# Norm sums behind the first products, recurrent value transposes one block later, and eight banks for the out blocks, in a two-layer hybrid encoder

## The chip, the core and the metric

The kernel runs on one core of a Trainium2 chip. A core has a matrix engine (TensorE, PE in the rows), three engines for element-wise work (VectorE: DVE; ScalarE: ACT; GpSimd: POOL), and SyncE (SP), which starts most of the transfers here. Each engine works through its own list of instructions in order, and waits there for what other engines or transfers have to deliver. TensorE writes its sums to PSUM, which has eight banks, and another engine has to read a bank out before it can take a new sum. What is measured is the time of one execution on the device, in microseconds; lower is better.

## The reference, cut to what matters

The model is an encoder of two layers (width 1024) on 656 tokens: one stream of 528 (16 learned meta tokens and 512 of the prompt) and eight running streams of 16. All is float32. Cut from the reference:

```python
h = rmsnorm(x, p['g_mix'])
proj = h @ p['w_in']                                   # 1024 -> 3072
qa, ka, va, glu, zf, ic, qc, gc = jnp.split(proj, offs, axis=-1)
oa = diff_attention(qa, k_all, v_all, ...)             # 4 heads
ob = jax.nn.silu(layernorm(causal_dwconv(ga * sigmoid(gb), ...)))   # 256 channels
oc, S_new = hgrn2(qc, log_f, kc, ic, S0)               # 4 heads, gated recurrence
x = x + jnp.concatenate([oa, ob, oc], axis=-1) @ p['w_out']
h2 = rmsnorm(x, p['g_ffn'])
gate, val = jnp.split(h2 @ p['w_up'], 2, axis=-1)      # 1024 -> 2 x 2816
gate_c, ffn_new = causal_dwconv(gate, ffn_past, ...)   # width 3
x = x + (jax.nn.gelu(gate_c) * val) @ p['w_down']      # 2816 -> 1024

def rmsnorm(x, g):
    return x * lax.rsqrt(jnp.mean(x * x, axis=-1) + EPS) * g
```

The factor `rsqrt(...)` of a token is the same for all columns of its row. A product can therefore be made from `x * g` before the factor is known, and be multiplied by it afterwards. The kernel calls this factor r.

## The kernel before, in words

Activations lie transposed, 128 features on the partitions and 656 tokens along the row, in two halves of 328 tokens (`CA`; 322 in the later stages of layer 1, `CB`). Float32 accuracy is reached by splitting each operand into a high and a low part and adding three products: high by high, high by low, low by high (`mm3`, three matmuls for each 128-row step). ScalarE makes the high part (a cast), VectorE the low part (a subtraction). For weights these are `whi`, `wlo` (four rotating buffers) or `ghi`, `glo` (buffers of their own); for activations `hi_h`, `lo_h`.

The sums in PSUM come from two pools of names: `PD` has three of the eight banks, `PB` five, and `PX` goes around all eight.

A layer starts with a group of six products (three column blocks by two halves, `gemm_group`, sums `e0` to `e5`), which need no r: r is applied when VectorE evicts them (`evict_r`). r itself comes from `norm_r`: VectorE and GpSimd add the squares of the eight blocks of x, TensorE sums these over the partitions (`np_h`, two matmuls of four passes in all), ScalarE takes the reciprocal root, and VectorE refines it in three steps (`rt_h`, twice, and `r_h`). 21 more column blocks follow one by one (`d_0_i03` and so on), and between them the attention heads (`attention`), the recurrent heads (`hgrn`, two pairs) and the convolution advance as generators: each `yield` hands on to the next block. In `hgrn` the values of a pair of heads are transposed on TensorE into the banks `hvp` and `hvq`.

Then comes the out projection in two passes, six of eight input blocks (`d_oa`) and the last two (`d_ob`). After each out block of the second pass VectorE adds the sum to x (`add_x`) and, between these additions, makes the splits of x for the FFN (`split`, `lo_h`).

The FFN starts with another group of six (`e_u`: two gates and one value block) and `norm_r` for its own r (`r_h2`). In `factors` the whole x is scaled by r on VectorE (eight blocks), GpSimd makes sums of quarters of it (`ft`, `fu`), and ScalarE and VectorE split these into factors (`fh`) for Strassen's scheme: seven products in place of eight for all later gates and values (`strassen`). The two gates of the group are evicted by `plain_gate` (`gp`), which frees banks `e0` to `e3`. Two more plain gates (`d_g02`, `d_g03`) with weights of their own (`wg`) and a value block (`d_v01`) stand ahead of the Strassen products (`d_v010` the first).

The program is written in the order of the blocks; a list scheduler lays out each engine's list from it, by what is ready and which bank or buffer is free. So the order of the source sets the order on the engines only in part, and the order of the lists is shown below where it matters.

Of the kernel before, what the change touches and what calls it, by code (L numbers as in the profile page):

```python
# [37 lines left out]
NPG = 2  # L38
# [9 lines left out]
CA, CB, CC = ((0, 328), (328, 656)), ((12, 334), (334, 656)), ((16, 336), (336, 656))  # L48
# [108 lines left out]
def trunk_kernel(ctx: ExitStack, tc: tile.TileContext, i: dict, o: dict, depth: int = 2):  # L157
# [14 lines left out]
    def S(name, dt=F32):  # L172
        return slots.tile([128, T], dt, tag="S", name=name)
# [4 lines left out]
    def PB(name):  # L178
        return psb.tile([128, 512], F32, tag="b", name=name)
# [29 lines left out]
    onesd = const.tile([128, 3, 128], F32, name="onesd")  # L209
# [93 lines left out]
    def norm_r(ones, srcs, nm, cc=CA):  # L303

        r = S(f"r_{nm}")
        t = S(f"rt_{nm}")
        for c, (a, b) in enumerate(cc):
            ps = PB(f"np_{nm}{c}")
            n = b - a
            for j, s in enumerate(srcs):  # L310
                PE.matmul(ps[:, :n], lhsT=ones, rhs=s[:, a:b], start=j == 0, stop=j == len(srcs) - 1)
            A.activation(out=r[:, a:b], in_=ps[:, :n], func=AF.Abs_reciprocal_sqrt, bias=epsb, scale=1.0)
            A.activation(out=t[:, a:b], in_=r[:, a:b], func=AF.Square)
            V.scalar_tensor_tensor(out=t[:, a:b], in0=ps[:, :n], scalar=EPS, in1=t[:, a:b], op0=ALU.add, op1=ALU.mult)
        a, b = cc[0][0], cc[-1][1]
        V.scalar_tensor_tensor(out=r[:, a:b], in0=t[:, a:b], scalar=-3.0, in1=r[:, a:b], op0=ALU.add, op1=ALU.mult)
        return r
# [47 lines left out]
    def weights(w, k0, kt, own=False):  # L365
        return w_split(w_load(w, k0, kt), kt, 0, own)
# [14 lines left out]
    def gemm(units, ks, rhs, nm, cc=CA, P=PD):  # L381

        return [gemm1(units, ks, rhs, f"{c}_{nm}", cc[c], P) for c in range(2)]

    def gemm_group(unit_lists, ks, rhs, nm, cc=CA):

        ps = [[PD(f"e0_{nm}"), PD(f"e1_{nm}")], [PD(f"e2_{nm}"), PB(f"e3_{nm}")], [PB(f"e4_{nm}"), PB(f"e5_{nm}")]]
        last = len(ks) - 1
        for k in range(len(ks)):
            for m, units in enumerate(unit_lists):  # L390
                for c in range(2):
                    mm3(ps[m][c], units[k], rhs[ks[k]], cc[c], k == 0, k == last)
        return ps

    def evict_r(ps, r, nm):
        t = SE(nm)
# [4 lines left out]
    sq_acc = {}  # L401
# [325 lines left out]
    def hgrn(l, p, got, mix):  # L727
# [3 lines left out]
        f = S(f"f{l}{p}")  # L731
# [7 lines left out]
        while ("i", p) not in got:  # L739
            yield  # L740
        iv = got["i", p]
        vt = S(f"hvt{l}{p}")
        ps = PB(f"hvp{l}{p}")
        for c in range(4):
# [57 lines left out]
        for c in range(2):  # L802
            ps = PB(f"hd{l}{p}{c}")
            PE.matmul(ps[:, :HC], lhsT=b64, rhs=prod[:, HV[c]], start=True, stop=True)
            V.scalar_tensor_tensor(out=od[:, HV[c]], in0=ps[:, :HC], scalar=64.0, in1=iv[:, HV[c]], op0=ALU.mult, op1=ALU.mult)
        ps = PB(f"hd{l}{p}2")
# [44 lines left out]
        ps = PB(f"hkp{l}{p}")  # L851
# [12 lines left out]
        for hh in range(2):  # L864
            pr = slice(64 * hh, 64 * hh + 64)
            ps = PB(f"hsi{l}{p}{hh}")
# [16 lines left out]
        ps = PB(f"hsc{l}{p}")  # L883
# [222 lines left out]
    ks8 = list(range(8))  # L1106
    for l in range(depth):
# [6 lines left out]
        got, mix = {}, {}  # L1114
        if l == 0:
            hs = []
# [8 lines left out]
            w3 = []  # L1125
            start["on"] = True
            for m in range(8):
                hs.append(split(xs[m], par("g_mix", m), f"h{l}{m}"))
                if m == 0:
                    w3 = [w_split(raws[n], 4) for n in range(3)]  # L1130
                if m == 3:
                    w3 = [w3[n] + w_split(raws[n], 8, 4, True) for n in range(3)]
            for m in range(8):
                sq_add(m, E=V)
            start["on"] = False
        r = norm_r(onesd[:, 0], [sq_acc["t"]], f"h{l}")
        ps3 = gemm_group(w3, ks8, hs, f"i{l}")
        with ExitStack() as behind:
            if l == 0:
                for e in (mybir.EngineType.DVE, mybir.EngineType.Activation):  # L1140
# [1 line left out]
            nxt = weights(w[col[3]], 0, 8)  # L1142
# [16 lines left out]
        for n in range(3, 24):  # L1159
            advance(front)  # L1160
            ps = gemm(nxt, ks8, hs, f"i{l}{n}")
            got[order[n]] = evict_r(ps, r, f"e{l}{n}")
            if n < 23:
                nxt = weights(w[col[n + 1]], 0, 8)
# [8 lines left out]
        cx, cy = (CB, CC) if l == depth - 1 else (CA, CA)  # L1173
        ka, kb = KORD[:6], KORD[6:]
# [3 lines left out]
        nxt = weights(wo[0], 0, 6)  # L1178
        for k in ka:
            mix[k] = split(*mix[k], f"mx{l}{k}")  # L1180
        for m in range(8):
            advance(front)
            x_in(m, xsrc)
            ps = gemm(nxt, ka, mix, f"oa{l}{m}", cx)
            add_x(m, ps, cx)
            nxt = weights(wo[m + 1], 0, 6) if m < 7 else weights(wo[0], 6, 2)
# [6 lines left out]
        hs = []  # L1193
        wu = i["w_up"][l]
        w3 = [weights(wu[n], 0, 8, True) for n in (0, 1, NFF)]
        for m in range(8):
            ps = gemm(nxt, kb, mix, f"ob{l}{m}", cx)
            add_x(m, ps, cx)
            x_out(m)
            sq_add(m, (cx[0][0], T))  # L1200
            hs.append(split(xs[m], par("g_ffn", 8 * l + m), f"h2{l}{m}", cx[0][0]))
            if m < 7:
                nxt = weights(wo[m + 1], 6, 2)
        r = norm_r(onesd[:, 0], [sq_acc["t"]], f"h2{l}", cx)
        ps3 = gemm_group(w3, ks8, hs, f"u{l}", cx)
        gout = S(f"gout{l}")[:, :NFF * 18].rearrange("p (f n) -> p f n", f=NFF)
        wd = i["w_down"][l]
        a0, cw = cy[0][0], cx[0][1] - cx[0][0]
# [11 lines left out]

        for ft in range(2):
            plain_gate(ft, ps3[ft])
        wg = [weights(wu[ft], 0, 8, True) for ft in range(2, 2 + NPG)]
        for ft in range(2):
            ps = ps3[2] if ft == 0 else gemm(weights(wu[NFF + 1], 0, 8), ks8, hs, f"v{l}1", cx, PB)
            a, av = gates.pop(ft)
# [120 lines left out]
        if l < depth - 1:  # L1347
            hs = []
            w3 = [weights(i["w_in"][l + 1][col[n]], 0, 8, True) for n in range(3)]
# [7 lines left out]
    ks = list(range(f0, f0 + nf))  # L1357
    wl = [weights(wd[m], f0, nf, True) for m in range(WA)]
    for c, (a, b) in enumerate(CF):
# [3 lines left out]
        for m in range(8):  # L1363
            if c == 0 and m < 8 - WA:
                wl.append(weights(wd[m + WA], f0, nf, True))
            ps = gemm1(wl[m], ks, gts, f"fin{c}{m}", (a, b))
# [5 lines left out]
        r = norm_r(onesd[:, 0], [sq_acc["t"]], f"fin{c}", ((a, b),))  # L1372
# [22 lines left out]
```

## Time and profile before

| | |
|---|---|
| median of 3 runs | 1721.53 us (1720.11 to 1721.71) |
| profiled execution | 1721.48 us, of which the span 1719.7 |
| TensorE busy | 1634.3 us, 95% |
| VectorE busy | 1320.1 us, 77% |
| ScalarE busy | 827.7 us, 48% |
| GpSimd busy | 573.0 us, 33% |
| mean granted TensorE clock | 0.983 of full |
| chain that ended last | TensorE 67%, VectorE 22%, issue 5% |

The span is the time from the first to the last instruction, and the rest of the execution lies around it. Busy times are sums over the span; an engine that is idle waits for a transfer or another engine. The chain follows the work that ended last back to the start, at each step to what released it, and gives the shares of the span by engine. The times in the rows below are counted from the start of the span. Layer 0 goes from 0 to about 865 us, its FFN from about 398.

### The profile page before, as it was taken

Reading aid. Unit: us, or ns where it says so; the run is one execution under the profiler, and the core shown is the slowest. Engines: PE = TensorE matmul, PEld = TensorE weight load, DVE = VectorE, ACT = ScalarE, POOL = GpSimd, SP = SyncE. Lnnn points to the kernel's source line nnn. Section 1 sums busy time; section 2 is a strip of 40 time slices with the busy share of each in tenths; the row PEclk is TensorE's granted clock in tenths of the full one; section 3 lists DMA queues with packets and bytes.
Section 4 is the critical chain, followed back from the end, with each engine's and each line's share of the span. In section 5 each row is a group of like instructions: output and inputs, shape, how many; then the busy total and the mean of one; then the engine's idle time right before and its main releaser. Section 6 shows DMA issues by size and latency. Waiting matters only on the chain.

```text
span 1719.7 us, 28451 instructions
## 1 busy us (share of the span) xinstructions
PE 1634.3 (95%) x10772; PEld 1535.7 (89%) x10772; DVE 1320.1 (77%) x2498; ACT 827.7 (48%) x1614; POOL 573.0 (33%) x614
## 2 busy tenths in 40 slices
PE   7999999999889999999999989899999999999997
PEld 6898878898889999999988978788999899999996
DVE  6579996769996696696747899966899967868765
ACT  6655565643553353343437536566545434334334
POOL 0103230007563353452211132200277534435413
PEclk9999999999999999999999999999999999999998
DMA  6222212242123322222412221213512232222212
GB/s 217 79 82 78 75 44 65 86 148 98 50 77 116 116 77 72 81 79 81 157 66 84 66 78 57 72 55 118 176 44 74 86 118 82 88 73 80 86 50 84
DMA packets 62330, 151.17 MB, mean 88 GB/s; under 512 B 11345, under 2 KB 16977, under 8 KB 62193
## 3 DMA queue, kind: packets, MB, share of 16 engines
q1 hardware_dynamic: 62192, 149.36, 26.5%
q8 instruction: 84, 1.38, 0.3%
q14 instruction: 54, 0.43, 0.1%
HBM read 129.80 MB, written 19.54 MB: 87 GB/s over the span
## 4 chain that ended last, share of the span: by engine, by line
PE 67%; DVE 22%; issue 5%; POOL 3%; ACT 2%; DMA 1%; SPq 0%; DVEq 0%; POOLq 0%; ACTq 0%
PE d_dn L373 16%; PE d_i L373 12%; PE d_v L373 11%; PE d_g L373 8%; PE d_oa L373 5%; DVE wlo L963 3%; DVE lo_g L332 2%; PE e_i L373 2%; DVE cva L688 2%; DVE wlo L360 1%; PE d_fin L373 1%; PE sc L490 1%; DVE ga L1085 1%; PE po L526 1%; DVE fh L1060 1%
## 5 line engine op out<-in xcount | busy, mean ns | idle before, releaser
L373 PE MATMUL d_v<-fh,whi 128*128 128x328 f32 (+1 forms) x1120 | 252.2, 312 | 1.2 <-ACT whi L962 1.2
L359 ACT CAST whi<-raw 128x384 fp32r<-128x384 f32 (+2 forms) x243 | 132.3, 547 | 246.0 <-PE d_i L373 77.9
L373 PE MATMUL d_g<-fh,whi 128*128 128x328 f32 (+1 forms) x1008 | 226.8, 312 | 0.0
L373 PE MATMUL d_i<-hi_h,whi 128*128 128x328 f32 x672 | 219.1, 326 | 0.0
L373 PE MATMUL d_i<-lo_h,whi 128*128 128x328 f32 x672 | 213.5, 318 | 0.0
L373 PE MATMUL d_i<-hi_h,wlo 128*128 128x328 f32 x672 | 212.9, 317 | 0.0
L373 PE MATMUL d_dn<-hi_g,wlo 128*128 128x328 f32 (+1 forms) x640 | 199.5, 312 | 6.1 <-DVE wlo L360 6.1
L373 PE MATMUL d_dn<-lo_g,whi 128*128 128x328 f32 (+1 forms) x640 | 199.0, 311 | 0.0
L373 PE MATMUL d_dn<-hi_g,whi 128*128 128x328 f32 (+1 forms) x640 | 198.4, 310 | 0.0
L360 DVE TENSOR_TENSOR wlo<-raw,whi 128x384 fp32r<-128x384 f32 (+2 forms) x243 | 167.8, 705 | 38.3 <-ACT whi L359 30.4
L373 PEld LDWEIGHTS d_v<-fh,whi 128*128 128x128 f32 x1120 | 189.4, 189 | 1.5 <-ACT whi L962 1.5
L373 PE MATMUL d_v<-fh,wlo 128*128 128x328 f32 (+1 forms) x560 | 176.7, 316 | 7.3 <-DVE wlo L963 6.7
L962 ACT CAST whi<-wcb 128x512 fp32r<-128x512 f32 x152 | 94.0, 620 | 164.5 <-PE d_dn L373 66.3
L373 PEld LDWEIGHTS d_g<-fh,whi 128*128 128x128 f32 x1008 | 170.5, 189 | 0.0
L373 PE MATMUL d_g<-fh,wlo 128*128 128x328 f32 (+1 forms) x504 | 158.6, 315 | 7.8 <-DVE wlo L963 7.8
L956 POOL TENSOR_TENSOR wcb<-raw 128x512 f32<-128x512 f32 x76 | 110.4, 1453 | 129.3 <-DMA raw<-in_w_up 80.0
L416 DVE TENSOR_TENSOR x<-d_dn,x 128x328 f32<-128x328 f32 (+1 forms) x112 | 55.1, 492 | 108.8 <-PE d_dn L373 107.3
L373 PEld LDWEIGHTS d_i<-hi_h,whi 128*128 128x128 f32 x672 | 127.4, 190 | 11.7 <-issue 7.0
L963 DVE TENSOR_TENSOR wlo<-wcb,whi 128x512 fp32r<-128x512 f32 x152 | 133.5, 878 | 4.3 <-ACT whi L962 3.7
L373 PEld LDWEIGHTS d_i<-lo_h,whi 128*128 128x128 f32 x672 | 127.4, 190 | 3.7 <-issue 1.9
L373 PEld LDWEIGHTS d_i<-hi_h,wlo 128*128 128x128 f32 x672 | 127.3, 190 | 1.7 <-issue 0.8
L373 PEld LDWEIGHTS d_dn<-hi_g,wlo 128*128 128x128 f32 x640 | 120.2, 188 | 7.7 <-DVE wlo L360 7.7
(383 smaller groups left out, 4124.1 us busy)
## 6 DMA issues: line engine op xcount, KB each, us to landing
raw<-in_w_up SPq DMA_DIRECT2D x88, 512.0 KB, 3.6
raw<-in_w_in SPq DMA_DIRECT2D x45, 512.0 KB, 3.6
raw<-in_w_down SPq DMA_DIRECT2D x48, 384.0 KB, 3.4
x_scr<-x SPq DMA_DIRECT2D x24, 328.0 KB, 2.6
x<-x_scr SPq DMA_DIRECT2D x24, 328.0 KB, 4.3
raw<-in_w_out SPq DMA_DIRECT2D x16, 384.0 KB, 3.2
x<-in_x SPq DMA_DIRECT2D x16, 328.0 KB, 5.6
cache_k<-in_cache_k SPq DMA_DIRECT2D x16, 256.0 KB, 4.2
```

Of the source, the lines that this page charges most:

```text
L332: V.tensor_tensor(out=lo[:, a:T], in0=src[:, a:T], in1=hi[:, a:T].bitcast(F32), op=ALU.subtract)
L359: seq(A.copy(hi[:, :n], raw[:, a:a + n]))
L360: seq(V.tensor_tensor(out=lo[:, :n], in0=raw[:, a:a + n], in1=hi[:, :n].bitcast(F32), op=ALU.subtract))
L373: PE.matmul(ps[:, :b - a], lhsT=ww[:, n], rhs=r[:, a:b], start=first and j == 0, stop=last and j == 2)
L416: V.tensor_tensor(out=xs[m][:, a:b], in0=ps[c][:, :b - a], in1=xs[m][:, a:b], op=ALU.add)
L490: PE.matmul(ps[:, o0:o0 + w], lhsT=q[64 * c:64 * c + 64, q0:q0 + 128], rhs=k[64 * c:64 * c + 64, n * w:(n + 1) * w], start=True, stop=True)
L526: PE.matmul(po[:, :128], lhsT=vt[:, j * 128:(j + 1) * 128], rhs=aT[:, j * 128:(j + 1) * 128], start=j == 0, stop=False)
L688: V.scalar_tensor_tensor(out=ap_, in0=up, scalar=wj, in1=ap_, op0=ALU.mult, op1=ALU.add)
L956: G.tensor_tensor(out=t, in0=x, in1=y, op=op)
L962: A.copy(hi, x)
L963: V.tensor_tensor(out=lo, in0=x, in1=hi.bitcast(F32), op=ALU.subtract)
L1060: V.tensor_tensor(out=lo, in0=x, in1=hi.bitcast(F32), op=ALU.subtract)
```

## The change

Four edits. In `gemm_group` the call of `norm_r` moves from ahead of the group to inside it, at the last step behind two of the three column blocks; this holds for the group of the input projection and for that of the FFN. In `hgrn` the value transposes of each pair of heads come one `yield` later. The out blocks of the second pass take their banks from `PX` in place of `PD`. The loads and splits of the weights for the two later plain gates move up, from behind the first two gates to behind the group.

```diff
-    def gemm_group(unit_lists, ks, rhs, nm, cc=CA):
+    def gemm_group(unit_lists, ks, rhs, nm, norm, cc=CA):
...
         for k in range(len(ks)):
             for m, units in enumerate(unit_lists):
+                if k == last and m == 2:
+                    r = norm_r(onesd[:, 0], [sq_acc["t"]], norm, cc)
                 for c in range(2):
                     mm3(ps[m][c], units[k], rhs[ks[k]], cc[c], k == 0, k == last)
-        return ps
+        return ps, r
...
         iv = got["i", p]
+        yield
         vt = S(f"hvt{l}{p}")
         ps = PB(f"hvp{l}{p}")
...
-        r = norm_r(onesd[:, 0], [sq_acc["t"]], f"h{l}")
-        ps3 = gemm_group(w3, ks8, hs, f"i{l}")
+        ps3, r = gemm_group(w3, ks8, hs, f"i{l}", f"h{l}")
...
-            ps = gemm(nxt, kb, mix, f"ob{l}{m}", cx)
+            ps = gemm(nxt, kb, mix, f"ob{l}{m}", cx, PX)
...
-        r = norm_r(onesd[:, 0], [sq_acc["t"]], f"h2{l}", cx)
-        ps3 = gemm_group(w3, ks8, hs, f"u{l}", cx)
+        ps3, r = gemm_group(w3, ks8, hs, f"u{l}", f"h2{l}", cx)
+        wg = [weights(wu[ft], 0, 8, True) for ft in range(2, 2 + NPG)]
...
         for ft in range(2):
             plain_gate(ft, ps3[ft])
-        wg = [weights(wu[ft], 0, 8, True) for ft in range(2, 2 + NPG)]
```

TensorE at the FFN's group of layer 0, before: `np_h200` and `np_h201` are the norm sums, `e0_u0` to `e5_u0` the group's sums, and the two digits behind `hi_h` end in the step of the product (0 to 7).

```order
L373 MATMUL e2_u0_4326<-hi_h202_4157,ghi_4060 128x328
L373 MATMUL e2_u0_4326<-lo_h202_4158,ghi_4060 128x328
L373 MATMUL e2_u0_4326<-hi_h202_4157,glo_4061 128x328
L373 MATMUL e0_u0_4324<-hi_h203_4187,ghi_4050 128x328
L311 MATMUL np_h200_4313<-sq0_4095,onesd_94 128x328
L311 MATMUL np_h201_4318<-sq0_4095,onesd_94 128x328
L373 MATMUL e3_u0_4327<-hi_h200_4097,ghi_4060 128x328
L373 MATMUL e3_u0_4327<-lo_h200_4098,ghi_4060 128x328
```

Here the norm sums come after three of the eight steps of the first products; the change takes them away from this place.

The same engine after the change, at the end of that group:

```order
L373 MATMUL e3_u0_4314<-lo_h207_4308,ghi_4064 128x328
L373 MATMUL e3_u0_4314<-hi_h207_4307,glo_4065 128x328
L311 MATMUL np_h200_4457<-sq0_4095,onesd_94 128x328
L311 MATMUL np_h201_4462<-sq0_4095,onesd_94 128x328
L373 MATMUL e4_u0_4315<-hi_h207_4307,ghi_4074 128x328
L373 MATMUL e4_u0_4315<-lo_h207_4308,ghi_4074 128x328
L373 MATMUL e4_u0_4315<-hi_h207_4307,glo_4075 128x328
```

The norm sums have moved from step 3 of the first products to step 7, behind 138 of the group's 144 matmuls.

VectorE at the same place, before, from the last low part of a weight to the scaling of x with r:

```order
L963 TENSOR_TENSOR wlo_4842<-raw_4837,whi_4841 128x512
L963 TENSOR_TENSOR wlo_4846<-raw_4837,whi_4845 128x512
L314 SCALAR_TENSOR_TENSOR rt_h20_4312<-np_h200_4313,rt_h20_4312 128x328
L314 SCALAR_TENSOR_TENSOR rt_h20_4312<-np_h201_4318,rt_h20_4312 128x328
L316 SCALAR_TENSOR_TENSOR r_h20_4311<-rt_h20_4312,r_h20_4311 128x656
L1038 SCALAR_TENSOR_TENSOR x0_3444<-x0_3444,cst_82,r_h20_4311 128x656
L1038 SCALAR_TENSOR_TENSOR x4_3834<-x4_3834,cst_82,r_h20_4311 128x656
L1038 SCALAR_TENSOR_TENSOR x1_3582<-x1_3582,cst_82,r_h20_4311 128x656
```

The three steps of r and the scalings stand one behind the other; the change puts others between them.

And after the change:

```order
L966 TENSOR_TENSOR wlo_4842<-raw_4837,whi_4841 128x512
L966 TENSOR_TENSOR wlo_4846<-raw_4837,whi_4845 128x512
L314 SCALAR_TENSOR_TENSOR rt_h20_4456<-np_h200_4457,rt_h20_4456 128x328
L360 TENSOR_TENSOR glo_4477<-raw_4474,ghi_4476 128x512
L314 SCALAR_TENSOR_TENSOR rt_h20_4456<-np_h201_4462,rt_h20_4456 128x328
L360 TENSOR_TENSOR glo_4481<-raw_4474,ghi_4480 128x512
L316 SCALAR_TENSOR_TENSOR r_h20_4455<-rt_h20_4456,r_h20_4455 128x656
L360 TENSOR_TENSOR glo_4487<-raw_4484,ghi_4486 128x512
L1041 SCALAR_TENSOR_TENSOR x0_3444<-x0_3444,cst_82,r_h20_4455 128x656
L360 TENSOR_TENSOR glo_4491<-raw_4484,ghi_4490 128x512
L1041 SCALAR_TENSOR_TENSOR x4_3834<-x4_3834,cst_82,r_h20_4455 128x656
L1041 SCALAR_TENSOR_TENSOR x1_3582<-x1_3582,cst_82,r_h20_4455 128x656
```

The instruction ahead of `rt_h20` is the same as before, and four low parts of the gates' weights (`glo`) now stand between the steps of r and the first scalings. The eviction of the first gate (`gp00`) has also moved, from behind the first eight `fh` to between the scalings and these.

TensorE in layer 0 behind the state updates of the first pair of recurrent heads (`hsu00`), before: `hvp01` and `hvq01` are the value transposes of the second pair, `np_qn01` the norm sums of a head's q, `tm_v01` and `tm2_v01` transposes of a head's values, `d_0_i015` a block of the input projection.

```order
L901 MATMUL hsu00_1822<-hvx000_1711,hkt00_1692 64x512
L901 MATMUL hsu00_1822<-hvx001_1718,hkt00_1692 64x512
L745 MATMUL hvp01_1830<-cst_82,e014_1774 128x128 x4
L747 MATMUL hvq01_1835<-cst_82,e014_1774 128x128
L748 MATMUL hvq01_1835<-cst_82,e014_1774 16x128
L311 MATMUL np_qn010_1844<-qsq01_1722,cst_82 128x328
L311 MATMUL np_qn011_1849<-qsq01_1722,cst_82 128x328
L429 MATMUL tm_v01_1857<-cst_82,e012_1567 128x128 x4
L431 MATMUL tm2_v01_1862<-cst_82,e012_1567 128x128
L432 MATMUL tm2_v01_1862<-cst_82,e012_1567 16x128
L373 MATMUL d_0_i015_1900<-hi_h00_132,whi_1779 128x328
```

The change takes the third to fifth of these rows away from this place.

And after the change, at the same place:

```order
L904 MATMUL hsu00_1822<-hvx000_1711,hkt00_1692 64x512
L904 MATMUL hsu00_1822<-hvx001_1718,hkt00_1692 64x512
L311 MATMUL np_qn010_1831<-qsq01_1722,cst_82 128x328
L311 MATMUL np_qn011_1836<-qsq01_1722,cst_82 128x328
L431 MATMUL tm_v01_1844<-cst_82,e012_1567 128x128 x4
L433 MATMUL tm2_v01_1849<-cst_82,e012_1567 128x128
L434 MATMUL tm2_v01_1849<-cst_82,e012_1567 16x128
L373 MATMUL d_0_i015_1887<-hi_h00_132,whi_1779 128x328
```

The transposes `hvp01` and `hvq01` have left this place; they stand one block of the input projection later, ahead of `sc01200`.

## Rows read from the trace of the kernel before

**Rows 1.** Windows: stretch; PE, PEld, DVE, ACT, POOL busy (count); clock; DMA share; GB/s.

```profile
400.00:430.00 30.00, 28.81 (x186) 27.96 (x186) 29.46 (x27) 8.15 (x17) 24.06 (x19) 1.00 0.09 30
430.00:459.00 29.00, 24.57 (x148) 23.80 (x149) 26.31 (x53) 18.97 (x36) 13.64 (x26) 0.94 0.18 55
460.00:860.00 400.00, 390.02 (x2566) 385.62 (x2565) 302.64 (x463) 165.29 (x278) 175.16 (x183) 1.00 0.29 93
```

**Rows 2.** TensorE's waits, whole span: who for whom, us in total, times, longest.

```profile
PE hvp L745 <- DVE e L398: 10.9, 4, 3.4
...
PE np_h L311 <- DVE sq L412: 8.0, 4, 3.6
...
PE d_ob L373 <- DVE x L416: 5.2, 4, 1.6
```

**Rows 3.** Timeline, TensorE, start of layer 0: start, duration, instruction, [idle before, releaser].

```profile
24.74 2.52 PE L311 MATMUL np_h<-sq,onesd 128*128 128x328 f32 x4 [2.84 <-DVE sq L412]
...
38.52 5.93 PE L287 MATMUL bps<-oh,rb 32*128 32x328 f32 x16
```

**Rows 4.** Timeline, TensorE, FFN entries of layer 0 and of layer 1.

```profile
399.88 0.41 PE L373 MATMUL e_u<-hi_h,ghi 128*128 128x328 f32 x1 [0.41 <-DVE x L416]
...
403.74 1.34 PE L311 MATMUL np_h<-sq,onesd 128*128 128x328 f32 x4 [0.90 <-DVE sq L412]
...
430.30 0.39 PE L373 MATMUL d_g<-hi_h,ghi 128*128 128x328 f32 x1 [0.59 <-DVE gp L1218]
...
458.70 0.42 PE L373 MATMUL d_v<-fh,wlo 128*128 128x328 f32 x1 [0.48 <-DVE wlo L963]
...
1249.65 1.32 PE L311 MATMUL np_h<-sq,onesd 128*128 128x322 f32 x4 [0.72 <-DVE sq L412]
```

**Rows 5.** Timeline, VectorE, FFN entry of layer 0.

```profile
406.57 0.50 DVE L314 SCALAR_TENSOR_TENSOR rt_h<-np_h,rt_h 128x328 f32<-128x328 f32 x1 [0.43 <-ACT rt_h L313]
...
407.11 1.31 DVE L316 SCALAR_TENSOR_TENSOR r_h<-rt_h,r_h 128x656 f32<-128x656 f32 x1
...
408.45 12.40 DVE L1038 SCALAR_TENSOR_TENSOR x<-x,cst,r_h 128x656 f32<-128x656 f32 x8
...
420.78 8.97 DVE L1060 TENSOR_TENSOR fh<-x,fh 128x328 fp32r<-128x328 f32 x8
...
429.67 1.83 DVE L1218 TENSOR_TENSOR gp<-e_u,r_h 128x328 f32<-128x328 f32 x6
...
457.96 0.68 DVE L963 TENSOR_TENSOR wlo<-raw,whi 128x512 fp32r<-128x512 f32 x1
```

**Rows 6.** Timeline, VectorE, boundary of the layers: first evictions of layer 1.

```profile
891.05 2.76 DVE L398 TENSOR_TENSOR e<-e_i,r_h 128x328 f32<-128x328 f32 x6 [14.82 <-PE e_i L373]
```

**Rows 7.** Timeline, TensorE, boundary of the layers.

```profile
871.06 2.42 PE L311 MATMUL np_h<-sq,onesd 128*128 128x328 f32 x4 [3.59 <-DVE sq L412]
```

**Rows 8.** Timeline, TensorE, layer 0, value transposes of the second recurrent pair.

```profile
173.48 0.69 PE L745 MATMUL hvp<-cst,e 128*128 128x128 f32 x2 [3.39 <-DVE e L398]
...
177.72 0.62 PE L373 MATMUL d_i<-hi_h,whi 128*128 128x328 f32 x1
```

**Rows 9.** Timeline, VectorE, the same place.

```profile
173.35 0.46 DVE L889 COPY hsall<-hs 64x64 f32<-64x64 f32 x2
173.84 2.46 DVE L893 SCALAR_TENSOR_TENSOR hsall<-hsall,tot,hsc 64x64 f32<-64x64 f32 x8
```

**Rows 10.** Timeline, VectorE, end of the out blocks, layer 0 and layer 1.

```profile
397.98 1.43 DVE L335 SCALAR_TENSOR_TENSOR lo_h<-x,cst,hi_h 128x656 fp32r<-128x656 f32 x1
...
399.34 0.49 DVE L416 TENSOR_TENSOR x<-d_ob,x 128x328 f32<-128x328 f32 x1
...
1243.18 0.88 DVE L416 TENSOR_TENSOR x<-d_ob,x 128x322 f32<-128x322 f32 x2
```

**Rows 11.** One tile, FFN entry of layer 0: ns min/median/max, first and last start.

```profile
L360 DVE TENSOR_TENSOR glo<-raw,ghi x4: 677/678/994, 432.5 to 437.6; 128x512 fp32r<-128x512 f32 x4
```

**Rows 12.** Timeline, VectorE, start of layer 0: the same shape with GpSimd idle.

```profile
29.99 0.84 DVE L316 SCALAR_TENSOR_TENSOR r_h<-rt_h,r_h 128x656 f32<-128x656 f32 x1
```

## The prediction

> **What bounds the kernel now.** I read the page's busy times and its chain first (the table above: TensorE leads both by far), then TensorE's waits, then the stages in windows, then the timelines of TensorE and VectorE at the places that the change touches. TensorE is the bound nearly everywhere: in a whole FFN stage of 400 us it is idle for 10 [rows 1]. Its waits are few and short. Three of the named ones are what this change goes for: 10.9 us of value transposes that wait for VectorE's eviction, 8.0 us of norm sums that wait for the last addition of squares, 5.2 us of out blocks that wait for a bank [rows 2]. The reader should also see the one stage where TensorE is not alone: from 400 to 430 us VectorE is busy for 29.46 of 30 us, and from 430 to 459 for 26.31 of 29, while TensorE loses 4.4 of those 29 [rows 1]. That is the entry of the FFN, and what comes late on VectorE there is late on TensorE.
>
> The profiled execution took 1721.48 us, 1719.7 of it the span; the median of the runs is 1721.53. So the sum is made on the profiled execution and set on 1721.5 without a correction. One matmul of the large products costs 0.152 us (390.02 us by 2566 of them [rows 1]).
>
> **Norm sums behind the first products, input projection.** In layer 0 TensorE idles 2.84 us for the sum of squares, then the clock is low: the four passes of the norm sums take 2.52 us [rows 3], against 1.34 us in another place [rows 4]. From there to the small bias products is 13.78 us [rows 3] for those and 72 matmuls, which at 0.152 and 1.34 would be 12.3. So 2.84 + 1.5 = 4.3 us go. The six products interleaved also fill the first microseconds, where TensorE waits for weights and activations; the rows do not price that, and I bound it by 0 and 3 us. What is late next is r: from the norm sums to the end of r is 4.7 us (403.74 to 407.11 + 1.31 [rows 4, 5]), and the first eviction is 0.5 more (2.76 by six [rows 6]), while TensorE has only six matmuls and the sums left, 0.9 + 1.3. All eight banks are held, so it waits 5.2 - 2.2 = 3.0 us. Net between -4.3 and +0.5 (a low clock after the new wait costs up to the 1.5 again); I take -3. At the boundary of the layers it is the same: 3.59 us of idle and 2.42 - 1.34 of slow sums go [rows 7], 3.0 come, and up to 1.5 of low clock: between -2.4 and 0, I take -1.5. VectorE has slack there, since it waits 14.82 us for TensorE before its six evictions [rows 6], so a late r hurts nobody else.
>
> **Value transposes one block later.** The second pair of heads waits up to 3.39 us at a time for the eviction of its values in layer 0 [rows 8]. In the new order the norm sums of q, the transposes of v (tm_v01, tm2_v01) and block d_0_i015 stand there instead. But tm_v01 takes the bank of hs000, and tm2_v01 that of hsc00, and VectorE reads those last in the copies and updates of hsall, which end at 173.84 and 176.30 [rows 9]. TensorE is in order, so d_0_i015 starts at about 176.7, against 177.72 [rows 8]. That is 1.0 us won, and the six transposes (about 1 us) are paid later, where sc01210 now also stands behind one more bank. VectorE sets the end in both orders. Between -1.5 and +1 a layer; I take +0.5, so +1 for two. The first pair of heads has no wait to lose.
>
> **All banks for out blocks.** TensorE would no longer stop at the third bank. But the additions into x are in order on VectorE between the splits (lo_h), which it does without a pause, and the last addition ends at 399.83 [rows 10]. The group behind it (e2_u0) takes the bank of the last out block, so it starts at 399.88 as it does now [rows 4]: the stalls move behind the block, and the gain is 0 in layer 0. In layer 1 e2_u1 needs only the first of the two additions that begin at 1243.18 [rows 10], so TensorE enters about 2 us earlier, which helps below. Bounds: -5.2 (all stalls go) to +1.5 (a low clock after one longer stall).
>
> The Trainium skill has a rule for this edit: by Perfetto Trace Analysis, section Optimizing Tensor Performance, independent matmul groups should rotate through different PSUM banks so that the evacuation of one overlaps the next, and its section Matmul Optimizations wants all 8 banks used. By that rule the sum below would be 5 us lower; the trace has VectorE without a pause while TensorE waits for it, so more banks let TensorE run ahead but not finish ahead.
>
> **Norm sums behind the first products, FFN entry.** This is the term that decides. Now the norm sums run at 403.74 [rows 4], after a few matmuls of the group; r is ready at 408.42, and VectorE goes straight into scaling x with r (12.40 us), the first eight factor splits fh (8.97), the six evictions of the gates (1.83), and on without slack to the low part of the weights for the fifth Strassen product, which TensorE waits for: VectorE ends it at 458.64, the matmul starts at 458.70 [rows 4, 5]. In the new order the sums stand behind 138 of the group's 144 matmuls, 128 of which come after the wait at 399.88: they run at 399.88 + 128 x 0.152 = 419.3, which is 15.6 us later. VectorE has nothing to fill that with: its order goes from lo_h207 and two wlo straight to rt_h20. Only the four low parts of the gates' weights (glo, 0.68 each [rows 11]) have moved up. Two stand between the steps of r (0.9 more, as 0.43 of idle is there already [rows 5]) and so 1.4 less behind; x0 and x4 lose the company of GpSimd's weight sums, for which I give 1.0 (a scaling takes 1.55 beside it, and an instruction of the same shape without it 0.84: `r_h` at 29.99 [rows 12]). Shift of the fifth product: 15.6 + 0.9 - 1.4 - 1.0 = 14.1 us. On TensorE it shows first at the bank of the first gate: TensorE gets there at 419.3 + 1.3 + 54 x 0.152 = 428.8, the eviction is done at 419.3 + 4.7 + 0.9 + 12.4 - 1.0 + 1.4 + 0.4 = 438.1, a wait of about 9 us (now 0.59 [rows 4]); then 4 to 5 at the second bank, and the rest at the fifth product. In layer 1 the group starts from 1243.65, 132 matmuls lie before the sums, 1263.7 against 1249.65 [rows 4]: 14.1 later, and 14.1 - 1.5 = 12.6 us. Together +26.7.
>
> What could cover it: if x were scaled at 0.84 instead of 1.55 throughout, 8 x 0.7 = 5.6 us a layer come back, so 7 to 8.5 is the low end of a layer's loss. With a low clock behind the waits 17 is the high end. I take the middle, since the new order leaves GpSimd's factor sums right behind the scalings, as now.
>
> **Sum.** -3 - 1.5 + 1 + 0 + 26.7 = +23.2, so 1721.5 + 23.2 = 1745 us.
>
> **Rivals.**
> 1. The waits simply go (faster). 10.9 + 8.0 + 5.2 = 24.1 us vanish, and the FFN entry costs little. Against it: VectorE has nothing to spare in the 60 us of the entry. For it: in the rest of the stage it is busy for 303 of 400 us [rows 1]. Time 1721.5 - 24.1 = 1697; it decides if r is not needed before the group ends. Chance 0.09.
> 2. The lateness is caught up inside the FFN stage (not slower). Place: the 400 us behind the entry. TensorE's 10 us of idle there [rows 1] are waits on VectorE; if VectorE gets ahead while TensorE is late, they go. Price: 2 x 10 back of 23, so 1725, and with VectorE's faster scaling 1718. It decides if those waits are the trail of the entry and not local. Chance 0.08.
> 3. Milder: x scaled quickly, or only the 9 us at the first gate's bank count: 7 to 9 a layer, 1721.5 - 3.5 + 16 = 1734. Chance 0.18.
> 4. The out blocks gain: VectorE's additions keep pace once TensorE runs ahead of them, so that the 5.2 us of stalls go: 1745 - 5 = 1740. Against it is VectorE's row without a pause. It is what the Trainium skill's rule on banks would give. Chance 0.10.
> 5. Worse: the clock falls in each new wait and the late entry makes later weights late too, 17 a layer: 1753. Chance 0.15.
>
> **How the numbers follow.** The forecast itself has 0.40, with 1739 to 1750 as its own range. What the measurement can tell from no change is about 0.2%, 3.4 us. Rival 1 is faster; half of rival 2 is within 3.4 us, the other half splits. So faster 0.11, same 0.05, slower 0.84. The range reaches from below the milder case, with the bounds of the start, the boundary and the transposes all on the good side (1734 - 6 = 1728), to the worse one with a margin, 1757.
>
> **What would show it.** Right: VectorE idle for some 14 us before r in both FFN entries, TensorE waiting about 9 us at the first gate for the gate's eviction, the waits of transposes, norm sums and out blocks gone from the list but d_0_i015 started less than 1.5 us earlier, with tm_v waiting on hsall, and a longer wait of the up group for x. The first d_0_i03 some 3 us earlier. Wrong: no wait at the first gate (then r was not what it waited for), or a fifth product less than 8 us later relative to the group's start.

## The result, and the profile after

The changed kernel takes 1749.60 us (median of 4 runs, 1749.29 to 1752.32) against 1720.82 (1719.76 to 1721.71): 1.0178 of before, 95% interval 1.0164 to 1.0191, or 28.8 us more. 1745 was forecast, 1728 to 1757 the range.

| | before | after |
|---|---|---|
| span of the profiled execution | 1719.7 us | 1747.5 us |
| TensorE busy | 1634.3 us, 95% | 1642.7 us, 94% |
| VectorE busy | 1320.1 us, 77% | 1309.2 us, 75% |
| mean granted clock | 0.983 | 0.972 |

To see where the time went, take VectorE's instructions of one kind (the evictions, the additions into x) in both traces, and set the n-th of the one beside the n-th of the other. The difference is how far the changed kernel is behind at that place:

| place (time before) | behind by |
|---|---|
| layer 0, projection, 160 us | -2.2 us |
| layer 0, behind the recurrent heads, 215 us | -0.2 |
| layer 0, out blocks, 381 to 399 us | -0.6 |
| layer 0, FFN, from 519 us | +13.3 |
| boundary of the layers: end of layer 0, first evictions of layer 1 | +12.8, +11.4 |
| layer 1, ahead of and behind the recurrent heads, 1016 and 1117 us | +11.3, +15.0 |
| layer 1, out blocks, 1228 to 1245 us | +15.0 |
| layer 1, FFN, from 1362 us | +28.1 |

So the loss is made at four places, the two FFN entries (13.9 and 13.1 us) and the two places of the recurrent heads (2.0 and 3.7); the start and the boundary give back 2.2 and 1.4.

Not all of this is shown to be the change's. In the kernel with late sums in the FFN's group alone (below), the lists of all four engines are those of before up to 380 us, and still its trace is 1.9 us ahead at 160 us. The kernel with late sums there and the gates' weights moved up has no edit at the boundary, and yet goes from 12.3 us behind to 10.7 there. In both, the norm sums ran faster behind the wait for the squares (the first line is from the one kernel, the second from the other):

```profile
24.55 1.70 PE L311 MATMUL np_h<-sq,onesd 128*128 128x328 f32 x4 [2.35 <-DVE sq L415]
...
883.35 1.37 PE L311 MATMUL np_h<-sq,onesd 128*128 128x328 f32 x4 [3.58 <-DVE sq L415]
```

The kernel before took 2.52 us at the first place [rows 3] and 2.42 at the second [rows 7], there with a granted clock of 0.55 in place of 1.00 (TensorE's clock has two levels, 1.2 and 2.4 GHz, granted 0.50 and 1.00). So the 2.2 and 1.4 are no more than what single traces differ by without the edit. Of the 3.7 in layer 1, 1.0 arises at 1111 us, where two kernels without an edit there (norm sums behind 72 matmuls; gates' weights behind each gate) lose 1.4 and 1.5. The losses at the FFN entries are far above this.

TensorE's waits show the same four places (columns as in [rows 2], whose three lines have all gone from this list):

```profile
PE d_g L373 <- DVE gp L1220: 12.8, 3, 6.8
PE tm_v L431 <- DVE hsall L892: 10.2, 2, 5.5
PE d_g L373 <- ACT fh L1062: 7.4, 1, 7.4
...
PE e_u L373 <- DVE x L418: 5.4, 3, 2.5
PE d_i L373 <- DVE e L400: 5.1, 2, 2.6
...
PE tm_v L433 <- DVE hsall L896: 2.8, 2, 1.4
```

Each wait that left has a successor at the same place: hvp by tm_v (10.9 by 13.0), the out blocks by the FFN's group (5.2 and 0.8 by 5.4), the norm sums by the first block behind the group (8.0 by 5.1). (`hsall` is VectorE's work on the recurrent state, which reads the sums `hs` and `hsc` out of their banks.) At the gates 20.2 us (12.8 + 7.4) stand in place of 5.4, which were, before:

```profile
PE d_g L373 <- DVE glo L360: 4.8, 2, 2.4
...
PE d_g L373 <- DVE gp L1218: 0.6, 1, 0.6
```

VectorE at the entry of the FFN in layer 0 (timeline; answers to [rows 5]; `gv` is the product of a value block with its gate `ga`, which GpSimd has scaled by r):

```profile
403.70 1.28 DVE L966 TENSOR_TENSOR wlo<-raw,whi 128x512 fp32r<-128x512 f32 x2
421.89 0.50 DVE L314 SCALAR_TENSOR_TENSOR rt_h<-np_h,rt_h 128x328 f32<-128x328 f32 x1 [16.91 <-ACT rt_h L313]
...
424.44 0.83 DVE L316 SCALAR_TENSOR_TENSOR r_h<-rt_h,r_h 128x656 f32<-128x656 f32 x1
...
425.79 0.89 DVE L1041 SCALAR_TENSOR_TENSOR x<-x,cst,r_h 128x656 f32<-128x656 f32 x1
...
427.21 9.52 DVE L1041 SCALAR_TENSOR_TENSOR x<-x,cst,r_h 128x656 f32<-128x656 f32 x7
436.65 0.76 DVE L1220 TENSOR_TENSOR gp<-e_u,r_h 128x328 f32<-128x328 f32 x2
437.34 8.18 DVE L1063 TENSOR_TENSOR fh<-x,fh 128x328 fp32r<-128x328 f32 x8
...
454.46 0.50 DVE L1233 TENSOR_TENSOR gv<-e_u,ga 128x328 f32<-128x328 f32 x1 [2.80 <-POOL ga L1228]
...
459.13 0.50 DVE L1233 TENSOR_TENSOR gv<-d_v,ga 128x328 f32<-128x328 f32 x1 [1.45 <-POOL ga L1228]
...
472.02 0.68 DVE L966 TENSOR_TENSOR wlo<-raw,whi 128x512 fp32r<-128x512 f32 x1
```

VectorE stands still for 16.9 us until r, in the one stretch where it had hardly any slack (3.2 of 59 us idle [rows 1]), and the low part of the fifth product's weights ends at 472.70, where the forecast's working gives 458.64 + 14.1 = 472.7. That this agrees to a tenth is luck, since two of its terms were off, in opposite directions (below). TensorE in the same stretch (answers to [rows 4]):

```profile
420.06 1.26 PE L311 MATMUL np_h<-sq,onesd 128*128 128x328 f32 x4
...
437.29 0.61 PE L373 MATMUL d_g<-hi_h,ghi 128*128 128x328 f32 x1 [7.36 <-ACT fh L1062]
...
445.86 0.39 PE L373 MATMUL d_g<-hi_h,ghi 128*128 128x328 f32 x1 [3.47 <-DVE gp L1220]
...
472.75 0.64 PE L373 MATMUL d_v<-fh,wlo 128*128 128x328 f32 x1 [2.68 <-DVE wlo L966]
```

The first of these waits is put down to a cast of ScalarE (`fh`) that this product does not read; the casts of its own weights (`ghi`) had ended by 424.7. What ended last for it is VectorE's eviction of the gate, which starts at 436.65, ends at 437.1 and frees the bank. In layer 1 the same wait has its right name (6.80 us for gp).

### The profile page after: what moved, and what is told of

It reads as the page before. It is cut to its first block, busy times and chain, and to the rows that moved or that the text cites. A ratio compares the mean times of both kernels' runs of the same rounds, so it can differ in the third digit from the quotient of the medians.

```text
span 1747.5 us, 28448 instructions
## 1 busy us (share of the span) xinstructions
PE 1642.7 (94%) x10772; PEld 1545.0 (88%) x10772; DVE 1309.2 (75%) x2498; ACT 827.0 (47%) x1614; POOL 565.0 (32%) x614
## 4 chain that ended last, share of the span: by engine, by line
PE 71%; DVE 22%; issue 3%; ACT 1%; POOL 1%; DMA 0%; DVEq 0%; SPq 0%; POOLq 0%; ACTq 0%
PE d_dn L373 16%; PE d_i L373 13%; PE d_v L373 11%; PE d_g L373 8%; PE d_oa L373 5%; PE e_i L373 2%; PE e_u L373 2%; DVE wlo L966 2%; DVE lo_g L332 2%; DVE fh L1063 2%; DVE cva L690 2%; DVE ga L1088 2%; PE sc L492 1%; PE d_fin L373 1%; DVE wlo L360 1%
## 5 line engine op out<-in xcount | busy, mean ns | idle before, releaser
L373 PE MATMUL d_v<-fh,whi 128*128 128x328 f32 (+1 forms) x1120 | 257.3, 316 | 7.0 <-ACT whi L965 3.3
```

What stands on the lines that cost most here:

```text
L373: PE.matmul(ps[:, :b - a], lhsT=ww[:, n], rhs=r[:, a:b], start=first and j == 0, stop=last and j == 2)
```

## Experiments

The ratio that stands first is to the kernel before on the same chip, with its 95% interval; a difference in us is that of the medians.

**The parts, one by one, in the kernel before.** First the norm sums late in the input projection's group alone:

```diff
+                if norm and (k, m) == (at or (last, 2)):
+                    r = norm_r(onesd[:, 0], [sq_acc["t"]], norm, cc)
...
-        r = norm_r(onesd[:, 0], [sq_acc["t"]], f"h{l}")
-        ps3 = gemm_group(w3, ks8, hs, f"i{l}")
+        ps3, r = gemm_group(w3, ks8, hs, f"i{l}", norm=f"h{l}")
```

> The kernel before with one part of the change: the norm sums late in the group of the input projection alone. Theory (the four edits add up, each worth what its place shows in the changed trace): VectorE's evictions 2.2 us earlier after the start, 1.4 more after the layers' boundary, so 1721 - 3.6 = 1717.5, and the waits of the later places as before. Rival (TensorE has no use of the earlier start, since VectorE sets the time at the recurrent heads and the out blocks in any case): the 2.2 us are gone by 215 us, and the time is 1719 to 1721.

0.9996 of before (0.9987 to 1.0005), 1718.94 us. No difference that can be told; the span is 2.5 us shorter in the one trace, with the evictions 1.2 us ahead at 160 us and 2.1 to 2.4 at the boundary. The norm sums' own waits go and 2.6 us of waiting for the first eviction come. The theory's 3.6 us lie outside the interval (-2.2 to +0.9 us). The rival's number lies inside, but its reason is not in the trace: the lead of 1.2 us is still 1.3 at 215 us, and at the start leads of that size come without the edit (above). What is left is a gain between nothing and 2.2 us.

The transposes alone:

```diff
         iv = got["i", p]
+        yield
         vt = S(f"hvt{l}{p}")
```

> The kernel before with one part of the change: the value transposes one block later. Theory (the bank of hs and hsc, which VectorE reads last, sets the time behind the first pair of heads, and the transposes are paid again later): tm_v waits on hsall for 5 to 6 us in place of hvp's 5.0 and 5.9, a new wait of hl of about 1 us, and 1.6 + 3.6 = 5.2 us more in the sum: 1726. Rival (the loss in the changed kernel came from TensorE reaching the place earlier and waiting longer, which cost nothing of its own): 1720 to 1722.

1.0029 (1.0019 to 1.0040), 1724.93 us, 5.0 us more: the theory. TensorE's waits for hsall are there without the rest of the change, in layer 0 and in layer 1 (timeline, start, duration, idle before):

```profile
173.04 1.09 PE L429 MATMUL tm_v<-cst,e 128*128 128x128 f32 x4 [4.66 <-DVE hsall L890]
175.53 0.45 PE L431 MATMUL tm_v<-cst,e 128*128 128x128 f32 x1 [1.41 <-DVE hsall L894]
...
209.42 0.79 PE L781 MATMUL hl<-qo,e 128*128 128x128 f32 x5 [1.15 <-DVE e L838]
...
1022.31 1.08 PE L429 MATMUL tm_v<-cst,e 128*128 128x128 f32 x4 [5.50 <-DVE hsall L890]
1024.80 0.45 PE L431 MATMUL tm_v<-cst,e 128*128 128x128 f32 x1 [1.41 <-DVE hsall L894]
```

The norm sums late in the FFN's group alone:

```diff
-        r = norm_r(onesd[:, 0], [sq_acc["t"]], f"h2{l}", cx)
-        ps3 = gemm_group(w3, ks8, hs, f"u{l}", cx)
+        ps3, r = gemm_group(w3, ks8, hs, f"u{l}", cx, f"h2{l}")
```

> The kernel before with one part of the change: the norm sums late in the FFN's group alone. Theory (r late on VectorE, which has no slack there): 13.9 + 13.1 = 27 us as in the changed kernel, up to 3 more as the low parts of the gates' weights stay behind the gates: 1748 to 1751. Rival (a part of the loss is the weights' low parts standing ahead of the scalings and the early loads): 8 x 0.68 = 5 us less, 1743.

1.0109 (1.0095 to 1.0123), 1738.97 us, 19.1 more. The largest part, but not the 27: the theory was wrong in size, and the rival's number (1743) is too high as well. VectorE waits nearly as long for r (15.47 us against 16.91), and then loses less, until TensorE starts the fifth product (last line):

```profile
418.82 0.50 DVE L314 SCALAR_TENSOR_TENSOR rt_h<-np_h,rt_h 128x328 f32<-128x328 f32 x1 [15.47 <-ACT rt_h L313]
...
431.48 0.76 DVE L1220 TENSOR_TENSOR gp<-e_u,r_h 128x328 f32<-128x328 f32 x2
...
440.42 1.16 DVE L360 TENSOR_TENSOR glo<-raw,ghi 128x512 fp32r<-128x512 f32 x1
...
450.95 0.50 DVE L1234 TENSOR_TENSOR gv<-d_v,ga 128x328 f32<-128x328 f32 x1 [0.35 <-POOL ga L1229]
...
465.59 0.54 PE L373 MATMUL d_v<-fh,wlo 128*128 128x328 f32 x1 [2.53 <-DVE wlo L966]
```

The low parts of weights (`glo`) stand where the changed kernel's VectorE waits 2.80 and 1.45 us for GpSimd, and that wait is 0.35 here.

All banks for the out blocks, alone:

```diff
-            ps = gemm(nxt, kb, mix, f"ob{l}{m}", cx)
+            ps = gemm(nxt, kb, mix, f"ob{l}{m}", cx, PX)
```

> The kernel before with one part of the change: all banks for the out blocks. Theory (VectorE's additions and splits in order end the stage): the stalls move to the first matmuls of the FFN's group, 0 us, 1721. Rival (the stalls go, as the named waits say): 5.2 us less, 1716.

1.0002 (0.9993 to 1.0010), 1719.62 us: nothing, as the theory has it. The 5 us of the rival are outside the interval. TensorE's stops have moved to the FFN's group, and behind them the granted clock is 1.00 (397.5 to 403):

```profile
397.57 0.41 PE L373 MATMUL e_u<-hi_h,ghi 128*128 128x328 f32 x1 [2.52 <-DVE x L416]
...
399.73 0.42 PE L373 MATMUL e_u<-hi_h,ghi 128*128 128x328 f32 x1 [0.85 <-DVE x L416]
```

The weights of the two gates moved up, alone:

```diff
+        wg = [weights(wu[ft], 0, 8, True) for ft in range(2, 2 + NPG)]
         gout = S(f"gout{l}")[:, :NFF * 18].rearrange("p (f n) -> p f n", f=NFF)
...
         for ft in range(2):
             plain_gate(ft, ps3[ft])
-        wg = [weights(wu[ft], 0, 8, True) for ft in range(2, 2 + NPG)]
```

> The kernel before with one part of the change: the weights of the two later gates moved up. Theory (the four low parts of weights are fillers: where they stood, VectorE had to wait for GpSimd's products of the gates anyway, and where they stand now they delay r and the scalings by 2.7 us): TensorE's wait of 2.4 us for the low part goes, the one for the gate's bank grows by as much, VectorE waits 2 to 4 us for GpSimd at gv, and the time is 2 to 6 us longer, 1722 to 1726. Rival (a wait for weights simply goes): 4.8 us less, 1715.

1.0032 (1.0021 to 1.0043), 1724.83 us, 5.4 more: the theory, and an edit that the forecast had booked as a gain. TensorE's waits in this kernel:

```profile
PE d_g L373 <- DVE gp L1219: 8.5, 4, 3.0
```

The 4.8 us for `glo` are gone, and 8.5 for the gates' banks stand in place of 0.6. VectorE's wait for GpSimd at gv is 3.9 us in place of 1.5. The profiled execution is the fastest of its runs, 2.1 us longer in its span; the other 3 us have no place in this trace.

**Two parts together.** The edits are those above.

> The kernel before with two parts: the norm sums late in the FFN's group, and the weights of the two gates moved up. Alone, the first gave 1739. Theory (the low parts of weights are missing as fillers behind the gates): 3 to 6 us more than the first alone, 1742 to 1745, with VectorE waiting for GpSimd at gv as in the changed kernel (2.8 and 1.5 us). Rival (what the whole change loses beyond its parts comes from the banks of the out blocks): 1739.

1.0152 (1.0135 to 1.0168), 1745.21 us: 25.7 us more than before, 6.6 more than late sums alone cost (19.1), a little over what the theory gave. VectorE's wait for GpSimd at gv:

```profile
DVE gv L1234 <- POOL ga L1229: 7.2, 4, 2.9
```

In the kernel with late sums alone the same line has 0.7 us, in the changed kernel 9.2.

> The kernel before with two parts: the norm sums late in the FFN's group, and all banks for the out blocks. Theory (TensorE waits in one piece at the group's start, the clock falls, and with late sums that delays r; with early sums it did not matter): r 1 to 1.5 us later than with late sums alone, 2 to 3 us in two layers, 1741 to 1742. Rival (the banks add nothing): 1739.

1.0129 (1.0111 to 1.0147), 1741.30 us. The size is that of the theory, but the interval overlaps that of late sums alone (1.0095 to 1.0123), so the banks' part of 2 to 3 us is not settled by the times. Its trace, at the start of the FFN's group:

```profile
395.13 0.41 PE L373 MATMUL e_u<-hi_h,ghi 128*128 128x328 f32 x1 [2.52 <-DVE x L419]
397.29 0.64 PE L373 MATMUL e_u<-hi_h,ghi 128*128 128x328 f32 x1 [0.84 <-DVE x L419]
```

After the second wait a matmul takes 0.64 and then 0.47 us in place of 0.31 for some 3 us: the clock is at its lower level (granted 0.50 from 397.5 to 400.5), and VectorE waits 17.02 us for r, 15.47 with late sums alone. The changed kernel has the lower clock there too. But with all banks alone the same two waits, 2.52 and 0.85 us, were followed by the full clock. So the one long wait does not bring the low clock in every trace, and its cause stays open.

**One part undone.** The changed kernel with `norm_r` back ahead of the FFN's group:

> The changed kernel with the norm sums of the FFN's group put back ahead of it; the three other edits stay. Theory (parts: input projection -0.8, transposes +5, banks 0, weights +5.4): 1729. Rival (late sums are the whole loss): 1720. Rival (the other edits only cost together with the late sums): 1723.

1.0041 (1.0027 to 1.0055), 1727.24 us: all but 6.6 of the 28.8 us go. The first theory's 1729 lies in the interval (1725.3 to 1730.1), the two rivals' numbers do not. What stays in that kernel (late sums in the input projection, transposes, banks, weights) keeps 6.6, where apart these come to 9.2 (5.0 + 5.4 - 0.9 - 0.3).

**How late r may be.** The late sums of the FFN's group alone, now behind 72 of the 144 matmuls:

```diff
-        r = norm_r(onesd[:, 0], [sq_acc["t"]], f"h2{l}", cx)
-        ps3 = gemm_group(w3, ks8, hs, f"u{l}", cx)
+        ps3, r = gemm_group(w3, ks8, hs, f"u{l}", cx, f"h2{l}", (4, 0))
```

> The kernel before with the norm sums of the FFN's group behind 72 of its 144 matmuls, so that r comes 5 us later in place of 15. Theory (VectorE's lateness is handed on in full but for what it gains when GpSimd's first weight sums no longer run beside the scalings): 1 to 3 us a layer, 1722 to 1726. Rival (loss in proportion to r's delay, 10 of 15): 3.5 us a layer, 1727. Rival (TensorE only needs r by the end of the group, so half way is free): 1720.

1.0036 (1.0023 to 1.0049), 1725.37 us. Against the group's start the sums run 5.6 us later than before (409.03 - 399.60 in place of 403.74 - 399.88), and the two layers cost 5.9 us. Half way is not free. In the one trace the two entries cost 0.7 and 1.5 us; the rest of its loss lies at places that the edit does not touch. Between the first theory and proportion the interval (4 to 8 us) does not decide.

**The bank behind the recurrent heads.** The later transposes again, with two sums in the other pool, so that `tm_v` and `tm2_v` get banks which VectorE read long ago:

```diff
         iv = got["i", p]
+        yield
...
-        ps0 = PB(f"hs0{l}{p}")
+        ps0 = PD(f"hs0{l}{p}")
...
-        ps = PB(f"hsc{l}{p}")
+        ps = PD(f"hsc{l}{p}")
```

> The kernel before with the value transposes one block later, and hs and hsc in banks of the other pool, so that tm_v and tm2_v take banks that VectorE has long read. Alone the later transposes gave 1725. Theory (the wait on hsall is a wait for the bank): no wait of tm_v on hsall; d_0_i015 waits for the eviction of d_1_i014 instead and starts 2 to 4 us earlier a layer; 1719 to 1722. Rival (VectorE's conv and state updates set the time behind this place whatever TensorE does): the wait goes but the time stays, 1725.

0.9987 (0.9978 to 0.9996), 1718.37 us: the wait was for the bank, and VectorE did not set the time. The same edit that costs 5 us gains 2 when two other tiles move. Two waits of hsc are left, 8.3 us in all, for 10.9 of hvp before, and d_0_i015 starts at 175.56 in place of 177.72 [rows 8] (0.9 us of it were there at 160 us), at the full clock (granted 1.00 from 175.5 to 178.2; with the transposes alone 0.50 from 173 to 178.7):

```profile
168.71 1.65 PE L887 MATMUL hsc<-hvt,hkt 128*128 128x128 f32 x6 [3.72 <-DVE e L398]
...
175.56 0.40 PE L373 MATMUL d_i<-hi_h,whi 128*128 128x328 f32 x1
```

**A better place for the gates' weights.** Each right behind the eviction of a plain gate:

```diff
+        wg = []
         for ft in range(2):
             plain_gate(ft, ps3[ft])
-        wg = [weights(wu[ft], 0, 8, True) for ft in range(2, 2 + NPG)]
+            wg.append(weights(wu[2 + ft], 0, 8, True))
```

> The kernel before with the weights of the first of the two later gates split right behind the eviction of the first plain gate, and those of the second behind the second. Theory (the low parts of weights have a place: behind the banks that TensorE waits for, ahead of the taps that wait for others): TensorE's wait for the low part falls from 2.4 to about 0.8 us a layer, 1.5 a layer, 1717. Rival (the end of the entry is set by VectorE's whole work up to the fifth product, which is the same): 1720.

1.0004 (0.9996 to 1.0013), 1720.37 us: the rival. The wait for `glo` falls from 4.8 to 2.2 us as wanted, and comes back at the gates' banks (0.6 to 2.5) and at the Strassen products (6.7 to 11.0):

```profile
PE d_v L373 <- DVE wlo L963: 11.0, 12, 2.1
...
PE d_g L373 <- DVE gp L1218: 2.5, 3, 1.0
PE d_g L373 <- DVE glo L360: 2.2, 2, 1.1
```

VectorE's whole work up to the fifth product sets the end of the entry, and this order, which leaves VectorE no more idle than before, only moves the places where TensorE waits. An order that makes VectorE wait is another matter, as the weights moved up show.

**What is left of the change.** Late sums in the input projection, and the later transposes with the two sums in the other pool:

> The kernel before with the two parts that did not lose: norm sums late in the input projection's group alone (0.9996 of before), and the transposes one block later with hs and hsc in banks of the other pool (0.9987). Theory (they lie at different places and add up): 0.9983 of before, 1717. Rival (the earlier start is lost at the recurrent heads, where VectorE sets the time): 0.9987, 1718.

0.9969 (0.9957 to 0.9981), 1715.44 us, 4.8 us less than before and the lowest median of all. It is more than the two parts give by their medians (0.9983, just outside this interval), and within what their intervals allow. The rival's 0.9987 is further outside.

## Why the prediction was right, and which terms were not

| term | forecast | changed trace | alone, by the runs |
|---|---|---|---|
| start of layer 0 | -3 us | -2.2 | with the next -0.9 (-2.2 to +0.9) |
| boundary | -1.5 | -1.4 | |
| transposes, both layers | +1 | +2.0 +3.7 | +5.0 |
| banks of the out blocks | 0 | 0 | -0.3 |
| FFN entries | +26.7 | +13.9 +13.1 | late sums 19.1, weights 5.4, together 25.7 |

**The term that decides** was right in place and in mechanism: r comes 17 us later, the first gate's bank is free at 437.1 (438.1 forecast), TensorE waits 7.4 and 6.8 us there (about 9 forecast), and the lateness is handed on to the fifth product. Putting the sums back alone takes 22 us out. That the size came out is luck in part. The forecast let VectorE's stretch from the first step of r to the fifth product shrink by only 1.5 us (1.0 for the scalings, 0.5 for `glo`), since VectorE goes "on without slack". Before, it starts here and ends at 458.70 [rows 4]:

```profile
405.64 0.50 DVE L314 SCALAR_TENSOR_TENSOR rt_h<-np_h,rt_h 128x328 f32<-128x328 f32 x1
```

| first step of r to fifth product | before | late sums alone | changed kernel |
|---|---|---|---|
| layer 0 | 53.1 us | 46.8 | 50.9 |
| layer 1 | 50.5 | 45.1 | 49.2 |
| VectorE idle in it, layer 0 | 3.2 | 0.9 | 5.4 |

Late sums alone give back 6.3 and 5.4 us of the lateness, and so cost 19.1 in place of 27. With the weights moved up as well, 4.1 a layer are lost again. The two errors nearly cancel, and 2.2 and 1.3 are left for the 1.5.

**The weights of the gates** were a step that failed inside it: "Two stand between the steps of r (0.9 more ...) and so 1.4 less behind". Moving them up is no gain of 0.5 a layer but a loss, 5.4 us alone and 6.6 on top of late sums. Behind the gates they filled time in which VectorE waits for GpSimd's product anyway (0.7 us of such waits with them there, 7.2 without), so taking them away there saves nothing. The other side of the sum is "without slack". With r late, GpSimd's weight sums run while VectorE waits, and the eight scalings take 0.89 + 9.52 us in place of 12.40 [rows 5], 2.0 less where 1.0 was allowed, and fh 8.18 in place of 8.97. With the weights left in place VectorE's idle time shrinks too.

**The transposes** were right in the wait (tm_v waits for hsall's banks) and in d_0_i015, which starts at 174.59 with everything 2.2 us earlier, so 176.8 on the old scale, where 176.7 was forecast. The steps that failed are "the six transposes (about 1 us) are paid later", as all that is paid behind it, and "VectorE sets the end in both orders". Behind the start of d_0_i015 layer 0 loses 3.0 us (from 3.1 ahead to 0.1): 1.0 while its matmuls run at the lower clock (granted 0.50 from 174.5 to 177.2), 0.7 with the transposes, and 1.3 with a new wait of hl, a product of the same heads (1.17 us; 1.03 in layer 1). In layer 1 the bank also costs more (5.5 + 1.4 against hvp's 2.5 + 3.4). With hs and hsc in the other pool the time falls from 1.0029 to 0.9987 of before, so VectorE did not set the end.

**The start** has its wait for r of 2.6 us (3.0 forecast), and the clock behind it at the lower level (granted 0.50 from 36 to 44.8). The bias products run wholly in it:

```profile
33.38 0.39 PE L373 MATMUL d_i<-hi_h,whi 128*128 128x328 f32 x1 [2.61 <-DVE e L400]
...
35.66 9.11 PE L287 MATMUL bps<-oh,rb 32*128 32x328 f32 x16
```

9.11 us in place of 5.93 [rows 3], where the clock fell only in their midst (granted 1.00 up to 41.6, 0.50 from 42): 3.2 us, twice what the bound of 1.5 allowed for the low clock. The start and the boundary together were to give 4.5 us; alone they give 0.9, and 4.5 is outside the interval.

**The out blocks** gave nothing, as forecast: all banks alone give 1.0002, and the wait has moved to the group's start (2.52 and 0.85 us), since the evicting engine is the later one. Together with late sums they may cost 2 to 3 us, which is not settled, and a part of the 13.9 in layer 0 may be theirs (12.3 with late sums and the weights moved up, without the banks). The Trainium skill's rule of rotating through different banks (Perfetto Trace Analysis, Optimizing Tensor Performance) speaks of evictions that overlap the next products. Here it has nothing to give.

Of the rivals, the faster one fails on its list: all three waits went, and the time rose. The catch-up did not happen either: from 519 to 862 us the lag goes from 13.3 to 12.8. The worse one (1753) is near in size, and its low clock is there in part: behind the wait at the first gate 0.50 is granted from 437.2 to 440, and over the whole TensorE is busy for 8.4 us longer, at a mean granted clock of 0.972 in place of 0.983.

## What to carry to other kernels

Before a step is moved to where its producer waits less, ask who is queued behind its consumer, and whether that engine has slack at the new time: the same late sums cost nothing that can be told where VectorE waits for TensorE, and 9 to 10 us a layer where it does not. A wait on a rotating bank is a wait for another tile's last reader, so moving one tile changes what its neighbours wait for; the cure may lie in the neighbours. Work that seems to stand in the way may be filling a hole. And a lag of one or two microseconds in a single trace is an effect only if traces without the edit do not have it.

## What the runs showed of the hardware

A wait of 2.6 us on TensorE, behind which 16 small products take 9.11 us at the lower clock level (5.93 where the clock fell in their midst), costs more than itself.

Equal waits are not followed by equal clocks. At the boundary ten traces have a wait of 3.57 to 3.59 us ahead of the same norm sums, which then take between 1.37 us (granted 1.00) and 2.56 us (granted 0.50).

A scaling on VectorE takes 0.89 us where GpSimd is idle, about 1.5 beside GpSimd's factor sums, and 1.81 and 1.94 beside its weight sums. With the weight sums out of the way the sixteen take 20.2 us, 24.1 before.
